# The end of a bidirectional scan and the start of its projection: side outputs of the last tile, the last scan unit and one tile's heads put at other places in the order

## The chip, the cores and the metric

The kernel runs on one core of one Trainium2 chip. The metric is the device time of one launch in microseconds (us); for the kernel before, three runs gave 2700.61, 2703.89 and 2706.90 us, so the median is 2703.89 us.

## What is computed

The reference is a small diffusion trunk with `DEPTH = 1`: 2048 latent tokens and 256 context tokens of width 1024 go through one HGRN2 mixer (a gated linear recurrence in both directions, 8 heads of 128) and one gated convolutional feed-forward block. Cut to what matters here:

```python
def hgrn2_chunk_scan(q, k, v, logf, s0):
    """S_t = diag(f_t) S_{t-1} + k_t v_t^T, o_t = S_t^T q_t"""
...
def hgrn2_mixer(h_ctx, h_lat, w_in, lb, g_gain, w_out, need_ctx):
    # q, zf_fwd, zf_bwd, v, g = split(h @ w_in, 5); f = lb + (1 - lb) * sigmoid(zf); k = 1 - f
    for d in range(2):
        oc_d, s_ctx = hgrn2_chunk_scan(... context, direction d, s0 = 0 ...)
        ol_d, _ = hgrn2_chunk_scan(... latents, direction d, s0 = s_ctx ...)
        o_l = o_l + _flip(ol_d, d, 2)
    def readout(o, g):
        o = rmsnorm(o, g_gain).transpose(0, 2, 1, 3).reshape(Bn, T, H * DV)
        return (o * jax.nn.silu(g)) @ w_out
...
lat = lat + g1 * yl
hl = modulate(rmsnorm(lat, norm_g[l, 1]), sh2, sc2)
lat = lat + g2 * conv_ffn(hl, ...)
return rmsnorm(lat, final_g)
```

So for each tile of 128 tokens and each head, the outputs of the two directions are added, normalised over the head's 128 values (sum of squares, power of minus one half, scale), multiplied by the silu of a gate, and the eight heads go through the output projection.

## The kernel before, in words

The latents are 16 tiles of 128 tokens (tiles 0 to 15). The scan (`mixer_scan`) runs over two groups `g` of eight tiles, in each over the eight heads `h`, and in each head over two units `u` of four tiles. The last thing that it does is therefore group 1, head 7, unit 1: tiles 12 to 15 of the last head.

**Ticks.** A projection of four tiles (512 columns) is eight steps of three matmuls (L943, L944, L945), each of 128 by 128 weights against 512 columns; the three are the high and low parts of a split product. One step is one tick of a clock. Everything else in the scan is put on an agenda, `at(tick, step)`, and is traced when the clock gets there. A head has two gate projections for each of its two units, 32 ticks in all. The last head has four more projections behind them (the output gates of heads 6 and 7, `out_gate`), so it has 64. Below, e+n is the n-th tick of head 7 in group 1. The traced order is not the last word: the compiler's scheduler orders each engine's instructions by its own cost model, and can issue a ready one ahead of one that it expects to wait. After that each engine takes its instructions strictly in order.

**A unit.** `gates` (ScalarE: L967, L969) makes the decay factors from a projection. `factors` then makes running products on VectorE (scans at L987; L998 to L1003) and small products on GpSimd (L1009 to L1031, `sd` at L1012 among them). At the ticks of the agenda follow `suffix` (two scans on VectorE, L1037, which wait for `sd`), `rest` (L1044 to L1052, L1021: the products `qp`, `qi`, `km`, `kd`, `ke` on VectorE), `scores` (TensorE: transposes of `kd` into the PSUM tag `tr`, L1075, and 48 small matmuls from `ke`, `km`, `qp`, L1119; then VectorE's masked copy L1136 and the sum `at` L1137), `stepped(0)` (matmuls `kv` L1150, states on VectorE L1153, copy `sk` on ScalarE L1158), `second` (`outputs(0)`, then `stepped(1)`) and `outputs(1)`. `outputs` writes `o` in PSUM (L1173 from the states, L1176 from `at`) and ScalarE copies it (`so`, L1181). The PSUM tag `o` has one buffer.

**Two directions.** The scan carries one direction's state (`Sf`) through the tiles. The other direction runs from tile 15 down to tile 0 in the projection phase (`mixer_out`): `heads(t)` multiplies the queries with the state `Sb` (`oi`, L841), adds to the stored output (L845), normalises, and moves `Sb` on by one tile (L852); `heads_T(t)` transposes, multiplies with the gates and splits (L880, L881, L80, L81); `residual(n, ...)` multiplies with the output weights (L1578 to L1580, 24 matmuls of 512 columns for each half). What passes from the scan to this phase goes through DRAM (`stash`), in four parts: state products `kv`, queries `q`, outputs and gates.

**Side outputs of tile 15.** For tile 15 the steps of `heads` and `heads_T` are done inside the scan, for heads 0 to 3, heads 4 and 5, and head 6 in turn, on data read back from the stash into one SBUF tile, `top`, with four parts (`kv`, `qb`, `o`, `g`):
- `load_top`: DMA from the stash (L1253, SP queue).
- `top_outputs`: matmuls `oi` (L1268) into the PSUM tag `o`, the one that the scan's own outputs use; VectorE adds it to `o` (L1270); ScalarE squares each head with a running sum, writing the squares over `oi` in PSUM (L1272); VectorE and GpSimd make the scale (L75, L76); VectorE moves `Sb` on (L1275).
- `top_scaled`: ScalarE multiplies by the scale (L1282).
- `top_turned`: transposes into the PSUM tag `tr` (L1289, also one buffer), VectorE's product with the gate (L1291), split (L80, L81).

Head 7 of tile 15 does the same in `last_out` and `last_turn`. `first_out` then holds tile 15's transposed and split outputs, and the projection phase begins with `residual(0, ...)` for tile 15, inside which `heads(14)` is traced.

Of the kernel before, what the change touches and what calls it, by code (L numbers as in the profile page):

```python
# [15 lines left out]
AF = mybir.ActivationFunctionType  # L16
# [29 lines left out]
def body(ctx, tc, a, out):  # L46
    nc = tc.nc
    pe, act, dve, pool, sp = nc.tensor, nc.scalar, nc.vector, nc.gpsimd, nc.sync
# [838 lines left out]
    clock, at, run, tick = ticking()  # L887
# [9 lines left out]
    def mixer_scan():  # L897
# [362 lines left out]
        def top_outputs(hs):  # L1260

            n, t = len(hs), NT - 1
            kv, qb, o, g = [top_part(i) for i in range(4)]
            ss, rs = [gp.tile([128, NH], F32, name=m, tag=m, bufs=2) for m in ("ss8", "rs8")]
            top_rs[hs] = rs
            oi = ps.tile([128, n, 128], F32, name="oi", tag="o")
            for j, h in enumerate(hs):
                pe.matmul(oi[:, j], qb[:, h], Sb[:, h], start=True, stop=True)  # L1268
            r = slice(hs[0], hs[-1] + 1)
            dve.tensor_tensor(o[:, r], o[:, r], oi, OP.add)  # L1270
            for j, h in enumerate(hs):
                act.activation(oi[:, j], o[:, h], AF.Square, accum_out=ss[:, j:j + 1])  # L1272
            rms_scale(rs[:, 0:n], ss[:, 0:n], n, 128)
            for h in hs:
                dve.scalar_tensor_tensor(Sb[:, h], Sb[:, h], decb[:, h, t:t + 1], kv[:, h],  # L1275
                                         OP.mult, OP.add)

        def top_scaled(hs):
            for j, h in enumerate(hs):
                o = top_part(2)[:, h]  # L1280
                with tc.issue_after(passed[-1]):
                    act.activation(o, o, AF.Copy, scale=top_rs[hs][:, j:j + 1])  # L1282

        def top_turned(hs):

            r = slice(hs[0], hs[-1] + 1)
            tp = ps.tile([128, len(hs), 128], F32, name="tp", tag="tr")
            for j, h in enumerate(hs):
                pe.transpose(tp[:, j], top_part(2)[:, h], ident)  # L1289
            g = top_part(3)[:, r]  # L1290
            dve.tensor_tensor(g, tp, g, OP.mult)  # L1291
            with tc.issue_after(passed[-1]):
                split(gls[0][:, r], gls[1][:, r], g)
# [45 lines left out]
        def head(g, h):  # L1339
            t0 = [HT * g, HT * g + UT]  # L1340
            last = g == 1 and h == NH - 1

            def ctx_gates():
                for d in range(2):
                    gates(d, h, None, project(weight(g, h, 2 - d), None))
                cv = values(cv_d[h // 2][:, h % 2])
                kd, sd, keys = factors(h, None, None, None, None)
                for dt, f in zip((5, 9, 12), (keys, *context_state(h, kd, sd, cv))):
                    at(clock[0] + dt, f)

            def gate(u):
                for d in range(2):
                    gates(d, h, u, project(weight(g, h, 2 - d), u))

            def unit(u, after):
                n = t0[u] // UT
                q = gp.tile([128, UT, 128], F32, name="q", tag="q", bufs=1)
                sp.dma_start(q, q_d[h][n])
                m, suffix, rest = factors(h, u, t0[u], q, values(v_d[h][n]))
                behind = (lambda: tied(rest)) if made_last else rest  # L1360
                for f, dt in zip((suffix, behind, *unit_steps(h, t0[u], m)), after):
                    at(clock[0] + dt, f)

            def out_gate(hh, u):
                keep_gate(hh, t0[u], swish(project(weight(g, hh, 4), u), ("q", "kdc")[hh % 2 ^ u]))

            if g == 0:
                ctx_gates()
            gate(0)
            unit(0, (6, 11, 19, 21, 24, 27) if last else (6, 11, 19, 21, 26, 31))  # L1370
            n = order.index((g, h)) + 1
            ahead = [(*order[n], ty) for ty in (2, 1)] if n < len(order) else \
                [(g, hh, 4) for hh in (NH - 2, NH - 1)]
            for i, w in enumerate(ahead):
                at(clock[0] + 2 + 7 * i, lambda w=w: weight(*w))
            gate(1)
            unit(1, (5, 9, 17, 19, 21, 23) if last else (6, 11, 19, 21, 26, 31))
            if last:
                c = clock[0]
                for k in range(4):  # L1380
                    at(c + 2 + k, lambda k=k: load_out_weight(k))
                for n, k in enumerate((4, 5, 6, 7)):
                    at(c + 8 + n, lambda k=k: load_out_weight(k))
                out_gate(NH - 2, 1)
                out_gate(NH - 2, 0)
                out_gate(NH - 1, 0)
                for k in range(4):
                    at(clock[0] + 1 + 2 * k, lambda k=k: split_out_weight(k))
                out_gate(NH - 1, 1)

        for g in range(2):
            for h in range(NH):
                c = clock[0]
                if g == 1 and h == 0:
                    tok.clear()
                    for kk, n in PLAIN.items():
                        sp.dma_start(block(*kk).bitcast(F32), tok_d[n])
                if g == 1 and h == 2:
                    at(c + 2, lambda now=c + 2: gate1(now))
                if g == 1 and 2 <= h < 6:  # L1400
                    for i in range(2):
                        at(c + 12 + 16 * i, lambda k=2 * (h - 2) + i, t=c + 12 + 16 * i: out_scaled(k, t))
                if g == 1 and h == NH - 2:
                    at(c + 36, lambda: load_top(range(6)))
                    for i, hs in enumerate(((0, 1, 2, 3), (4, 5))):
                        at(c + 44 + 10 * i, lambda hs=hs: top_outputs(hs))
                        at(c + 55 + 11 * i, lambda hs=hs: top_scaled(hs))
                        at(c + 65 + 9 * i, lambda hs=hs: top_turned(hs))
                if g == 1 and h == NH - 1:
                    hs = (NH - 2,)  # L1410
                    at(c + 35, lambda: load_top(hs, range(3)))
                    at(c + 42, lambda: top_outputs(hs))
                    at(c + 50, lambda: top_scaled(hs))
                    at(c + 48, lambda: load_top(hs, (3,)))
                    at(c + 57, lambda: top_turned(hs))
                head(g, h)
# [125 lines left out]
    def mixer_out(c3):  # L1542
# [128 lines left out]
        for t in range(NT - 1, -1, -1):  # L1671
            lat = next_lat
            steps = ()
            if prev is not None:
                xn = wn.tile([128, D], F32, name="xn", tag="xn", bufs=1)
                if t == NT - 2:
                    with behind_of(last_split[-1]):
                        steps = norm_steps(prev, xn)
                else:
                    steps = norm_steps(prev, xn)  # L1680
            if 1 < t < NT - 1:
                heads(t - 2, steps)
            else:
                for f in steps:
                    f()
            if 0 < t < NT - 1:
                next_lat = load_lat(t - 1)
            g = gs.pop(0)
            if t == NT - 1:
                residual(0, lat, *g, between={3: lambda: heads(t - 1)})  # L1690
                next_lat = load_lat(t - 1)
            else:
                residual(0, lat, *g, between={KT - 1 if t == NT - 2 else 1: turn} if t else {})
            if t == 1:
                load_rhs(1, "T2")
                for p in first:
                    p.load()
            if t == 0:
                for q, p in enumerate(first):
                    p.split("A11", hp.tile([128, 2, 4, 128], F32R, name="w", tag=("Sf", "Sb")[q],  # L1700
                                           bufs=1))
            residual(1, lat, *g, between={5: turn} if t == NT - 1 else
                     {} if t else {1: lambda: norm2(1, xn)})
            if t == NT - 1:
                heads(t - 2)
                sp.dma_start(conv[:, 0:V_CN], a["conv"])
            if t == 0:
                load_rhs(1, "T1")
            if prev is not None and t:
                norm2(t + 1, xn)  # L1710
            sp.dma_start(lat_d[t], lat)
            prev = lat
# [550 lines left out]
```

## Time and profile before

| what | value |
|---|---|
| median of three runs | 2703.89 us |
| the profiled execution's own time | 2705.35 us |
| its span (first to last instruction) | 2703.5 us |
| TensorE's mean granted clock | 0.995 |
| head 7 of group 1 begins (first step) | about 1124.3 us into the span |
| first matmul of the projection of tile 15 | 1203.56 us into the span |

All positions below are in us from the start of the span. A row of the timeline gives start, duration, engine, line, operation, out<-in, shapes, how often (merged), and in square brackets the engine's idle time before the row and what ended it. The view of waits gives who waited for whom, the total, the number of waits and the longest. The view of windows gives, for a stretch, its length and for each engine the busy time (and instructions), then the granted TensorE clock (PEclk), DMA's share and its GB/s.

### The profile page before, as it was taken

The numbers are of one execution on the slowest core, as the hardware profiler recorded it, in microseconds if no ns is written. First come the engines' busy times: TensorE is split into PE (matmuls) and PEld (weight loads), VectorE is DVE, ScalarE is ACT, GpSimd is POOL, SyncE is SP. The second block draws the span as 40 slices with busy tenths as digits, with TensorE's granted clock in tenths as the row PEclk, the third lists the DMA queues.
The fourth block names the chain that finished last, engine by engine and source line by source line (L and its number), as shares of the span: only waits on it lengthen the run. The fifth ranks groups of instructions, "written<-read, shape, count | busy, mean of one in ns | idle before, by whom it ended". The sixth has DMA issues, their size and how long they took to land.

```text
span 2703.5 us, 42065 instructions
## 1 busy us (share of the span) xinstructions
PE 2646.1 (98%) x15800; PEld 2205.9 (82%) x15800; DVE 2074.4 (77%) x2953; ACT 1187.3 (44%) x2051; POOL 597.9 (22%) x934
## 2 busy tenths in 40 slices
PE   7899999999999999999999999999999999999998
PEld 4787788888888888888887888888888888888887
DVE  4856766667887889878887878877887777578896
ACT  4645534433333233345566444443444444333444
POOL 1000222321222121111112444334433440000001
PEclk9999999999999999999999999999999999999999
DMA  8755655363445665548887322227232224888653
GB/s 341 276 198 195 233 197 183 102 248 120 151 152 175 217 204 180 163 138 310 294 315 278 107 81 94 86 71 296 94 94 68 86 81 159 301 283 285 206 180 133
DMA packets 257915, 498.12 MB, mean 184 GB/s; under 512 B 28192, under 2 KB 141232, under 8 KB 249136
## 3 DMA queue, kind: packets, MB, share of 16 engines
q1 hardware_dynamic: 252992, 486.20, 52.5%
q10 hardware_dynamic: 4720, 9.24, 0.9%
q8 instruction: 124, 2.03, 0.3%
q14 instruction: 79, 0.65, 0.1%
HBM read 335.70 MB, written 159.66 MB: 183 GB/s over the span
## 4 chain that ended last, share of the span: by engine, by line
PE 72%; DVE 10%; DMA 3%; POOL 1%; ACT 1%; issue 1%; SPq 0%; POOLq 0%; DVEq 0%; ACTq 0%
PE y L2076 4%; PE y L2075 4%; PE y L2077 4%; PE z L943 3%; PE z L945 3%; PE z L944 3%; PE zc L1474 3%; PE zc L1476 3%; PE zc L1477 3%; PE zd L1476 3%; PE za L1476 3%; PE za L1477 3%; PE zd L1477 3%; PE zd L1474 3%; PE za L1474 3%; PE y L1580 2%
## 5 line engine op out<-in xcount | busy, mean ns | idle before, releaser
L80 ACT ACTIVATE w<-raw 128x512 fp32r<-128x512 f32 (+1 forms) x286 | 186.1, 656 | 215.9 <-PE zd L1477 75.0
L81 DVE TENSOR_TENSOR w<-raw,w 128x512 fp32r<-128x512 f32 (+1 forms) x286 | 226.8, 797 | 64.3 <-ACT w L80 61.8
L81 DVE TENSOR_TENSOR w<-s,w 128x512 fp32r<-128x512 f32 x195 | 173.0, 892 | 81.8 <-ACT w L80 80.2
L2075 PE MATMUL y<-w,mh 128*128 128x512 f32 x600 | 233.4, 390 | 0.6 <-ACT X L2109 0.6
L2076 PE MATMUL y<-w,mh 128*128 128x512 f32 x600 | 233.5, 389 | 0.2 <-DVE w L81 0.2
L2077 PE MATMUL y<-w,ml 128*128 128x512 f32 x600 | 233.4, 389 | 0.0
L80 ACT ACTIVATE w<-s 128x512 fp32r<-128x512 f32 x195 | 121.7, 630 | 204.8 <-POOL s L220 82.5
L76 POOL TENSOR_TENSOR rs<-rs,mhalf 128x1 f32<-128x1 f32 (+3 forms) x53 | 58.2, 1102 | 446.5 <-DVE rs L75 433.9
L943 PE MATMUL z<-tok,w 128*128 128x512 f32 x352 | 145.6, 414 | 0.0
L1474 PE MATMUL zc<-rT,w 128*128 128x512 f32 x352 | 137.1, 389 | 1.9 <-DMA rT<-rhs1T 1.9
L945 PE MATMUL z<-tok,w 128*128 128x512 f32 x352 | 138.5, 394 | 0.0
L944 PE MATMUL z<-tok,w 128*128 128x512 f32 x352 | 138.0, 392 | 0.0
L1158 ACT ACTIVATE sk<-kv 128x256 f32<-128x256 f32 x64 | 24.6, 384 | 256.4 <-DVE states L1153 121.1
L1476 PE MATMUL zc<-rT,w 128*128 128x512 f32 x352 | 137.0, 389 | 0.0
L1477 PE MATMUL zc<-rT,w 128*128 128x512 f32 x352 | 136.9, 389 | 0.0
L219 POOL TENSOR_TENSOR s<-raw 128x512 f32<-128x512 f32 x54 | 90.6, 1677 | 194.9 <-DMA raw<-in_w_up_dram 128.7
L2075 PEld LDWEIGHTS y<-w,mh 128*128 128x128 f32 x600 | 112.6, 188 | 24.9 <-ACT X L2109 1.5
L2076 PEld LDWEIGHTS y<-w,mh 128*128 128x128 f32 x600 | 112.6, 188 | 23.8 <-DVE w L81 0.6
L2077 PEld LDWEIGHTS y<-w,ml 128*128 128x128 f32 x600 | 112.6, 188 | 23.6
L1476 PE MATMUL za<-rB,w 128*128 128x512 f32 x336 | 130.7, 389 | 0.0
L1477 PE MATMUL za<-rB,w 128*128 128x512 f32 x336 | 130.7, 389 | 0.0
L1474 PE MATMUL za<-rB,w 128*128 128x512 f32 x336 | 130.7, 389 | 0.0
(466 smaller groups left out, 7750.9 us busy)
## 6 DMA issues: line engine op xcount, KB each, us to landing
raw<-in_w_up_dram SPq DMA_DIRECT2D x88, 512.0 KB, 3.5
raw<-in_w_in_dram SPq DMA_DIRECT2D x75, 512.0 KB, 5.2
w<-w SPq DMA_DIRECT2D x32, 1024.0 KB, 6.1
lr<-m SPq DMA_DIRECT2D x49, 512.0 KB, 4.6
m<-r SPq DMA_DIRECT2D x66, 256.0 KB, 3.5
spare<-in_w_ada_dram SPq DMA_DIRECT2D x32, 512.0 KB, 5.1
kq<-stash SPq DMA_DIRECT2D x15, 1024.0 KB, 7.1
og<-stash SPq DMA_DIRECT2D x30, 512.0 KB, 5.1
```

What stands on the lines that cost most here:

```text
L80: i = act.activation(h, src, AF.Copy)
L81: j = dve.tensor_tensor(l, src, h.bitcast(F32), OP.subtract)
L219: eng.tensor_tensor(s1, a21, a22, OP.add)
L943: pe.matmul(z, w[:, 0, k], h, start=k == 0, stop=False, skip_group_check=True)
L944: pe.matmul(z, w[:, 0, k], l, start=False, stop=False, skip_group_check=True)
L945: pe.matmul(z, w[:, 1, k], h, start=False, stop=k == KT - 1, skip_group_check=True)
L1474: pe.matmul(o, w[:, 0, k], r[:, :, 0, k], start=start and k == 0, stop=False, skip_group_check=True)
L1476: pe.matmul(o, w[:, 0, k], r[:, :, 1, k], start=False, stop=False, skip_group_check=True)
L1477: i = pe.matmul(o, w[:, 1, k], r[:, :, 0, k], start=False, stop=k == 3, skip_group_check=True)
L2075: pe.matmul(z, lh, rh, start=start, stop=False, skip_group_check=True)
L2076: pe.matmul(z, lh, rl, start=False, stop=False, skip_group_check=True)
L2077: pe.matmul(z, ll, rh, start=False, stop=stop, skip_group_check=True)
```

## The change

No operation is added or taken away, and one operand changes. There are four edits:
1. `top_outputs` writes its squares over the query part of `top` in SBUF instead of over `oi` in PSUM.
2. The agenda of the side outputs moves: `top_outputs` is put two ticks behind the scan's own `outputs(1)`.
3. The last unit (head 7, unit 1) gets scores, states and outputs three ticks sooner.
4. `heads(14)` is traced behind the weights' second k-tile of tile 15's first half projection instead of behind the fourth.

In ticks of head 7:

| step | before | after |
|---|---|---|
| `outputs(1)` of head 6, unit 0; unit 1 | e+15; e+31 | e+15; e+31 |
| `top_outputs` heads 0-3; 4, 5; 6 | e+12; e+22; e+42 | e+17; e+33; e+45 |
| `top_scaled` | e+23; e+34; e+50 | e+28; e+39; e+51 |
| `top_turned` | e+33; e+42; e+57 | e+38; e+45; e+57 |
| `outputs(1)` of head 7, unit 0 | e+43 | e+43 |
| head 7, unit 1: scores; `stepped(0)`; `second`; `outputs(1)` | e+49; e+51; e+53; e+55 | e+46; e+48; e+50; e+52 |

```diff
             dve.tensor_tensor(o[:, r], o[:, r], oi, OP.add)
             for j, h in enumerate(hs):
-                act.activation(oi[:, j], o[:, h], AF.Square, accum_out=ss[:, j:j + 1])
+                act.activation(qb[:, h], o[:, h], AF.Square, accum_out=ss[:, j:j + 1])
             rms_scale(rs[:, 0:n], ss[:, 0:n], n, 128)
...
-            unit(1, (5, 9, 17, 19, 21, 23) if last else (6, 11, 19, 21, 26, 31))
+            unit(1, (5, 9, 14, 16, 18, 20) if last else (6, 11, 19, 21, 26, 31))
...
                     for i, hs in enumerate(((0, 1, 2, 3), (4, 5))):
-                        at(c + 44 + 10 * i, lambda hs=hs: top_outputs(hs))
-                        at(c + 55 + 11 * i, lambda hs=hs: top_scaled(hs))
-                        at(c + 65 + 9 * i, lambda hs=hs: top_turned(hs))
+                        at(c + 49 + 16 * i, lambda hs=hs: top_outputs(hs))
+                        at(c + 60 + 11 * i, lambda hs=hs: top_scaled(hs))
+                        at(c + 70 + 7 * i, lambda hs=hs: top_turned(hs))
...
-                    at(c + 42, lambda: top_outputs(hs))
-                    at(c + 50, lambda: top_scaled(hs))
+                    at(c + 45, lambda: top_outputs(hs))
+                    at(c + 51, lambda: top_scaled(hs))
                     at(c + 48, lambda: load_top(hs, (3,)))
...
-                residual(0, lat, *g, between={3: lambda: heads(t - 1)})
+                residual(0, lat, *g, between={1: lambda: heads(t - 1)})
```

In the first block of the agenda c is the start of head 6 (c + 32 is e), in the second it is e itself.

## The prediction

> **What bounds the kernel now.** I read the page first, then the view of waits for TensorE over 1110 to 1240 us, then each engine's timeline there.
>
> ```profile
> PE 2646.1 (98%) x15800; PEld 2205.9 (82%) x15800; DVE 2074.4 (77%) x2953; ACT 1187.3 (44%) x2051; POOL 597.9 (22%) x934
> ```
>
> TensorE (PE) is busy for 98% of the span and the change neither adds nor removes a matmul. So the time can move only by TensorE's idle time or by its clock. Its waits in the touched stretch:
>
> ```profile
> PE o L1173 <- ACT oi L1272: 3.9, 2, 3.0
> PE y L1578 <- ACT ghl L80: 1.4, 1, 1.4
> PE o L1176 <- DVE at L1137: 0.6, 1, 0.6
> PE tp L880 <- DVE og L866: 0.3, 1, 0.3
> ```
>
> The first is the largest: twice the scan's own outputs waited until ScalarE had squared the side outputs, because `oi` held the only buffer of the PSUM tag `o`. The longer wait, engine by engine:
>
> ```profile
> 1142.02 0.39 PE L943 MATMUL z<-tok,w 128*128 128x512 f32 x1
> 1145.82 0.49 PE L1173 MATMUL o<-states,qi 128*128 128x128 f32 x2 [2.95 <-ACT oi L1272]
> ...
> 1149.04 0.63 PE L943 MATMUL z<-tok,w 128*128 128x512 f32 x1
> ```
> ```profile
> 1141.42 0.32 DVE L1153 SCALAR_TENSOR_TENSOR states<-states,sd,kv 128x128 f32<-128x128 f32 x1
> ...
> 1143.31 0.68 DVE L1270 TENSOR_TENSOR top<-top,oi 128x512 f32<-128x512 f32 x1
> ```
> ```profile
> 1145.58 0.19 ACT L1272 ACTIVATION_READ_ACCUMULATOR oi<-top 128x1 f32 x1
> ```
>
> The last state that the outputs need was there at 1141.74. The buffer came free only at 1145.77, after VectorE's add and four squares. TensorE lost 2.95 us. The matmul at 1149.04 shows a second loss: 0.63 us where the same one takes 0.39 at 1142.02. The windows say why (PEclk is the number behind the five busy times):
>
> ```profile
> 1146.00:1148.00 2.00, 2.00 (x12) 1.76 (x13) 0.87 (x1) 1.97 (x6) 1.02 (x1) 0.80 0.01 2
> 1148.00:1150.00 2.00, 2.00 (x6) 1.54 (x6) 1.30 (x4) 0.56 (x2) 1.55 (x7) 0.50 0.66 195
> 1150.00:1152.00 2.00, 2.00 (x87) 1.63 (x89) 1.57 (x2) 0.60 (x1) 0.58 (x4) 0.85 0.00 0
> ```
> ```profile
> 1219.00:1223.00 4.00, 3.26 (x21) 2.76 (x22) 3.63 (x6) 2.63 (x5) 0.00 (x0) 1.00 1.02 418
> ```
>
> The granted clock was 0.80, 0.50 and 0.85 of full speed in the six microseconds behind the wait, which costs 0.4 + 1.0 + 0.3 = 1.7 us. Behind the wait of 1.4 us (the second of the list, which ends at 1219.67) it stayed at 1.00. So a long wait costs more than itself.
>
> **The change part by part.** The sum is made against the profiled execution: span 2703.5 us, its own time 2705.35, so 1.85 lies around the span, and it ran 1.46 us above the median of 2703.89. I apply the difference to the median.
>
> *Side outputs behind the scan's outputs (first group).* Outputs at e+15 now come before `oi` at e+17 and need only the state of 1141.74, about when TensorE ends the step that began at 1142.02. The 2.95 us go, and with them the clock's 1.7: **4.65 us**. The new danger is that `oi` waits for the copy `so`, which must empty the same buffer. It has two steps (1.36 us, by the rows below) for a copy of 256 columns; a gate's 0.60 us instruction could slip ahead of it. I take 0, with 0.5 as the bad end. The add, the `Sb` updates and the power go behind the next unit's `factors`: on GpSimd the power (L76) then stands behind that unit's small products instead of ahead. `top_outputs`, `top_scaled` and `top_turned` issue no DMA, so no SP instruction moves with them.
>
> *Third group (head 6).* The other part of that wait, 3.9 - 2.95, stands here, before `outputs(1)` at e+43:
>
> ```profile
> 1183.68 0.49 PE L1173 MATMUL o<-states,qi 128*128 128x128 f32 x2 [0.93 <-ACT oi L1272]
> ```
>
> With `oi` at e+45 it has nothing to wait for on ScalarE: **0.93 us**, without a clock dip (a shorter wait than the 1.4 us that had none).
>
> *Squares to SBUF.*
>
> ```profile
> L1282 ACT ACTIVATE top<-top,rs 128x128 f32<-128x128 f32 x7 | 2.3, 391 | 0.0
> L1272 ACT ACTIVATE oi<-top 128x128 f32<-128x128 f32 x7 | 2.0, 281 | 2.4 <-DVE top L1270 2.3
> ...
> L1300 ACT ACTIVATE y<-o 128x128 f32<-128x128 f32 x1 | 0.3, 277 | 0.1
> ```
>
> A square into PSUM takes 281 ns, the one square into SBUF (L1300, reading PSUM) 277, a scaled copy from SBUF to SBUF 391. So one square changes by -0.004 to +0.11 us, seven by at most 0.8. I take 0, because L1300 is the same operation; it is ScalarE time that TensorE no longer waits for. The Trainium skill speaks against this edit (ScalarE: Activation LUTs, Step-by-step: what each stage is for): it says ScalarE reaches PSUM faster than SBUF and advises PSUM as the destination. By it the bad end would hold, 0.8 us less gain if VectorE's L75, which waits for the squares in its queue, passed all of it on; the 277 against 281 does not bear it out.
>
> *The last unit three ticks sooner.* This is where the change can lose. Here is the stretch from e+32 on, first TensorE, then ScalarE, VectorE and GpSimd:
>
> ```profile
> 1166.44 0.60 PE L1289 MATMUL tp<-ident,top 128*128 128x128 f32 x4
> 1166.79 0.48 PE L943 MATMUL z<-tok,w 128*128 128x512 f32 x1
> ...
> 1168.27 0.60 PE L1075 MATMUL tr<-ident,kd 128*128 128x128 f32 x4
> ...
> 1170.49 0.48 PE L943 MATMUL z<-tok,w 128*128 128x512 f32 x1
> ...
> 1171.96 1.05 PE L1150 MATMUL kv<-v,kt 128*128 128x128 f32 x8
> 1172.77 0.48 PE L943 MATMUL z<-tok,w 128*128 128x512 f32 x1
> ...
> 1174.23 0.39 PE L943 MATMUL z<-tok,w 128*128 128x512 f32 x1
> 1174.91 0.38 PE L1173 MATMUL o<-top,qi 128*128 128x128 f32 x2
> ```
> ```profile
> 1165.94 0.60 ACT L967 ACTIVATE F<-z 128x512 f32<-128x512 f32 x1 [0.31 <-PE z L945]
> ```
> ```profile
> 1167.07 0.69 DVE L1291 TENSOR_TENSOR top<-tp,top 128x512 f32<-128x512 f32 x1 [3.00 <-PE tp L1289]
> ...
> 1169.79 0.68 DVE L81 TENSOR_TENSOR gh<-top,gh 128x512 fp32r<-128x512 f32 x1
> 1171.43 2.48 DVE L1037 TENSOR_TENSOR_SCAN S<-F,d 128x528 f32<-128x528 f32 x2 [0.96 <-POOL sd L1012]
> ...
> 1181.98 0.68 DVE L1021 TENSOR_TENSOR ke<-ke,rt 128x512 f32<-128x512 f32 x1
> ```
> ```profile
> 1158.21 3.41 POOL L76 TENSOR_TENSOR rs<-rs,mhalf 128x2 f32<-128x2 f32 x1 [7.57 <-DVE rs L75]
> ```
>
> The scores need `ke`. From the gate's start (1165.94, the projection of e+32) to the end of `ke` (1182.66) the chain over ScalarE, VectorE and GpSimd takes 16.7 us. TensorE's own work from e+32 to e+46 is 14 steps of 0.68 (1174.23 to 1174.91) = 9.5; the scores of unit 0, 2.22 (1168.27 to 1170.49); two `kv` and two `outputs` of eight 128-column matmuls, 4 x 0.81 (1171.96 to 1172.77) = 3.24; `oi` of heads 4 and 5, the transposes of heads 0 to 3, and `oi` of head 6 with the transposes of 4 and 5, 0.35 each (1166.44 to 1166.79) = 1.05. That is 16.0 us. So the slack that e+49 had is used up: the scores come 0.7 us too early if nothing else changes. And 0.69 + 0.68 = 1.37 us of VectorE work, the gate product and split of heads 0 to 3, leave a place with 3.00 us of idle time and come (e+38) into this chain: 2.1 us too early. Against it, TensorE can take steps ahead: at 1142.02 it did the 16th step before outputs due at the 15th, and three steps of the scores' former lead (2.0 us) have no other dependence. So this costs 0 to 2.1; I take **-0.5**. The work of heads 4 and 5 at e+33 (add, two `Sb` updates) fits into the idle 3.00 and 0.96 us. Behind the scores the spacing is the old one. The DMAs of the moved steps (two of `sk`, two of `so` on ScalarE's queue, two of `qi` on SP's) go 2 us sooner and pass no load.
>
> The wait for `at` (0.59 us, the third of the list) shrinks by the 0.35 us of `oi` for heads 4 and 5, which TensorE now does before it: **0.35 us**.
>
> *Heads of tile 14 sooner.*
>
> ```profile
> 1203.24 0.32 SPq L1550 DMA_DIRECT2D kq<-stash  x1
> ```
> ```profile
> 1203.56 0.39 PE L1578 MATMUL y<-wo,gh 128*128 128x512 f32 x1
> ...
> 1208.98 1.95 PE L841 MATMUL oi<-Sb,kq 128*128 128x128 f32 x16
> ...
> 1219.67 0.50 PE L1578 MATMUL y<-wo,ghl 128*128 128x512 f32 x1 [1.39 <-ACT ghl L80]
> ```
> ```profile
> 1198.53 0.37 ACT L1302 ACTIVATE y<-o,rs 128x128 f32<-128x128 f32 x1
> 1198.80 0.27 ACT L1181 ACTIVATE so<-o 128x128 f32<-128x128 f32 x1
> 1198.95 0.60 ACT L974 ACTIVATE kdc<-z 128x512 f32<-128x512 f32 x1
> ```
>
> `heads(14)` was traced behind the fourth k-tile, yet its `oi` ran only 5.4 us into the projection, twice the 2.7 us that the 12 matmuls of four k-tiles take (0.68 for three), because `kq` was only issued at 1203.24. Tracing it behind the second k-tile by itself gives nothing: **0**. What moves `kq` is the gate of head 7, unit 0, whose buffer it reuses. Its sigmoid (1198.95) stood behind the last unit's scaled output and copy, 0.37 + 0.27 us, and these now come three ticks sooner. So the heads' chain, on which the 1.4 us and 0.3 us waits of the second tile hang, can gain 0 to 0.64 us: **0.4**.
>
> Sum: 4.65 + 0.93 - 0.5 + 0.35 + 0.4 = **5.8 us**; 2703.89 - 5.8 = **2698.1 us** (2699.5 beside the profiled execution).
>
> **The rivals.**
> *The wait moves into the last unit's chain (slower).* One mechanism: GpSimd's power for heads 4 and 5, now traced right behind `factors` of unit 1, is issued ahead of that unit's small products, which `sd` and all of the chain wait for. Its price is the 3.41 us of the row at 1158.21. With 2.1 from above TensorE waits 5.5 us before the scores, and the clock dips as it did (1.7): 7.2. Against that stand 4.65 + 0.93 + 0.4, so the kernel is 1.2 us slower: 2705.1. It decides from a wait of 4.3 us on. For it: VectorE already idles 0.96 us for `sd` there. Against it: the traced order puts the small products first.
> *TensorE waits for `kq`.* If `oi` really stands behind the second k-tile, it is due at 1203.56 + 6 x 0.227 = 1204.9 and waits up to 4.1 us, with a dip of 1.7; the second tile's 1.4 + 0.3 are then gone. 4.1 less gain: 2702.2. Against it: the order followed the data before.
> *The dip is not the wait's.* Then only waits go: 5.8 - 1.7 = 4.1, 2699.8. For it: one place alone shows it here; against it: the clock falls right behind this wait and not behind the one of 1.4 us. The Trainium skill has the rule for it (TensorE: Matmul & The Clock Gate, Part 1: The HAM clock gate): half clock after an idle window of about 3.4 us, and by that a wait of 2.95 should leave the clock alone. This trace does not agree, with 0.50 behind 2.95 us.
> *More goes.* If also `at` (0.6) and the second tile's waits (1.4 + 0.3) vanish and the scores wait for nothing: 4.65 + 0.93 + 0.6 + 1.7 = 7.9, 2696.0.
>
> **How the numbers follow.** A measurement of this kernel can tell about 0.2% (5.4 us) from no change, so the line is at 2698.5. Chances: the forecast 0.50, with its own range 2696 to 2700 from the ends of the small terms, two thirds of it beyond the line (0.34); more goes 0.14; the chain 0.12, half of it worse than worked out, if unit 0's chain suffers too (0.06 slower); `kq` 0.12; the dip 0.06; no effect for another reason 0.06. Faster 0.34 + 0.14 = 0.48, slower 0.06, within 0.46. The range goes from 2694 (the largest gain and the 3 us by which runs differ from their median, in part) to 2703.5; beyond it lie the chain and half of no effect.
>
> **What would show it.** Right: no wait of L1173 for L1272; PEclk 1.00 through the scan's tail; the first projection matmul about 5.5 us earlier than 1203.56. Wrong: a wait before the last unit's L1075 or L1119 over 2 us, with L1037 waiting for `sd` longer than 0.96; a wait before L841; L1268 waiting for L1181; a second dip.

## The result and the profile after

The kernel after takes 2698.94 us in the median of 15 runs, the kernel before 2703.89 us in 15 runs beside them. The ratio is 0.9984 with a 95% interval of 0.9977 to 0.9990, so the change saves 4.3 us (2.7 to 6.2). The forecast was 2698.1 us. The profiled execution of after took 2697.74 us, with a span of 2695.8. One execution of after (9427.12 us), one of squares_only (4609.63) and the profiled one of later (2935.69) stand far outside all others, for a reason that no run shows, and are in no ratio and no reading below.

The page of after, first its busy times: TensorE's work is the same 15800 instructions, its busy time is 2.8 us less.

```profile
PE 2643.3 (98%) x15800; PEld 2205.0 (82%) x15800; DVE 2072.6 (77%) x2953; ACT 1188.0 (44%) x2051; POOL 599.6 (22%) x934
```

TensorE's waits from 1100 to 1240 us in after (who waits for whom: total, how often, the longest):

```profile
PE y L1578 <- ACT ghl L80: 1.4, 1, 1.4
PE tr L1075 <- ACT kt L1077: 0.5, 1, 0.5
PE o L1173 <- DVE states L1153: 0.4, 1, 0.4
PE tp L1289 <- ACT kt L1077: 0.3, 1, 0.3
```

The wait of L1173 for L1272 (3.9 us in two places) is gone, and so are those for `at` (0.6) and for `og` (0.3). Three waits are new, 0.5, 0.4 and 0.3 us. TensorE's timeline of after, at the places where those waits stood:

```profile
1138.27 0.38 PE L1173 MATMUL o<-states,qi 128*128 128x128 f32 x2
...
1140.84 1.05 PE L1268 MATMUL oi<-Sb,top 128*128 128x128 f32 x8
...
1145.51 0.66 PE L1075 MATMUL tr<-ident,kd 128*128 128x128 f32 x4 [0.52 <-ACT kt L1077]
...
1173.47 0.49 PE L1173 MATMUL o<-states,qi 128*128 128x128 f32 x2 [0.41 <-DVE states L1153]
```

The scan's outputs run without a wait, and the side outputs' `oi` follows 2.57 us behind them. The windows behind that place (PEclk is the number behind the five busy times) show the full clock, also in the third (1150 to 1152, 1.00), where before had 0.80, 0.50 and 0.85:

```profile
1146.00:1148.00 2.00, 2.00 (x14) 1.73 (x13) 2.00 (x3) 0.60 (x1) 1.43 (x1) 1.00 0.00 0
1148.00:1150.00 2.00, 2.00 (x13) 1.71 (x12) 1.93 (x4) 0.00 (x0) 0.00 (x0) 1.00 0.00 0
...
```

To compare executions I measure between four matmuls that every kernel has, so that what an execution loses elsewhere stays out: the first step of head 7 (e, at 1125.09 in before; the step at 1124.31 is still the last one of head 6), the step e+32, the first matmul of the projection (P15), and the first of tile 11's projection (P11). TensorE's timeline of after has them here:

```profile
1122.20 0.40 PE L943 MATMUL z<-tok,w 128*128 128x512 f32 x1
...
1158.51 0.40 PE L943 MATMUL z<-tok,w 128*128 128x512 f32 x1
...
1195.34 0.39 PE L1578 MATMUL y<-wo,gh 128*128 128x512 f32 x1
...
1258.48 0.48 PE L1578 MATMUL y<-wo,ghl 128*128 128x512 f32 x1
```

And in before (its P15 is the row at 1203.56 above):

```profile
1125.09 0.40 PE L943 MATMUL z<-tok,w 128*128 128x512 f32 x1
...
1165.74 0.40 PE L943 MATMUL z<-tok,w 128*128 128x512 f32 x1
...
1267.09 0.48 PE L1578 MATMUL y<-wo,ghl 128*128 128x512 f32 x1
```

From e to P11 before took 142.00 us and after 136.28: 5.72 us less. The same differences in all traces, in us ("dip" says that the clock fell to half for a while in that piece):

| kernel | edits in it | e to e+32 | e+32 to P15 | P15 to P11 | sum |
|---|---|---|---|---|---|
| before | none | 40.65, dip | 37.82 | 63.53 | 142.00 |
| before_again | none | 40.69, dip | 37.81 | 63.18 | 141.68 |
| heads_only | 4 | 39.22 | 37.80 | 63.31 | 140.33 |
| unit_only | 3 | 40.64, dip | 37.73 | 63.13 | 141.50 |
| squares_only | 1 | 38.59 | 37.61 | 63.56 | 139.76 |
| top_only | 2 | 35.87 | 36.92 | 64.19 | 136.98 |
| no_unit | 1, 2, 4 | 36.31 | 36.90 | 64.00 | 137.21 |
| no_squares | 2, 3, 4 | 35.86 | 36.82 | 63.28 | 135.96 |
| no_heads | 1, 2, 3 | 36.31 | 36.83 | 63.18 | 136.32 |
| after | 1 to 4 | 36.31 | 36.83 | 63.14 | 136.28 |
| later_again | 1 to 4, `oi` later | 36.54 | 36.80 | 65.26, dip | 138.60 |
| lat_first | 1 to 4, `lat` first | 36.29 | 36.82 | 66.97, dip | 140.08 |
| lat_mid | 1 to 4, `lat` second | 36.30 | 36.82 | 65.09, dip | 138.21 |

Executions of one order agree within 0.05 us in the first two columns, once a dip is set apart, and within about 0.35 us in the third (63.18 to 63.53 for before's order). Differences of some tenths can be read from this table; no timing of the whole kernel could show them.

### The profile page after: what moved, and what is told of

It is laid out like the page before. It is cut to its first block, busy times and chain, and to the rows that moved or that the text cites. A ratio compares the mean times of both kernels' runs of the same rounds, so it can differ in the third digit from the quotient of the medians.

```text
span 2695.8 us, 42069 instructions
## 1 busy us (share of the span) xinstructions
PE 2643.3 (98%) x15800; PEld 2205.0 (82%) x15800; DVE 2072.6 (77%) x2953; ACT 1188.0 (44%) x2051; POOL 599.6 (22%) x934
## 4 chain that ended last, share of the span: by engine, by line
PE 53%; DVE 1%; DMA 1%; issue 0%; ACT 0%; POOL 0%; SPq 0%; POOLq 0%; DVEq 0%; ACTq 0%
PE y L2076 5%; PE y L2077 5%; PE y L2075 5%; PE zc L1474 3%; PE zc L1477 3%; PE zc L1476 3%; PE za L1477 3%; PE zd L1477 3%; PE zd L1474 3%; PE zd L1476 3%; PE za L1476 3%; PE za L1474 3%; PE y L1580 2%; PE y L1578 2%; PE y L1579 2%; PE zb L1477 1%
## 5 line engine op out<-in xcount | busy, mean ns | idle before, releaser
L76 POOL TENSOR_TENSOR rs<-rs,mhalf 128x1 f32<-128x1 f32 (+3 forms) x53 | 57.4, 1086 | 431.2 <-DVE rs L75 407.3
L1474 PE MATMUL zc<-rT,w 128*128 128x512 f32 x352 | 137.6, 391 | 2.2 <-DMA rT<-rhs1T 2.2
L1474 PE MATMUL za<-rB,w 128*128 128x512 f32 x336 | 130.7, 389 | 0.0
```

The costliest lines, as they stand in the source:

```text
L1474: pe.matmul(o, w[:, 0, k], r[:, :, 0, k], start=start and k == 0, stop=False, skip_group_check=True)
```

## The experiments

The theory when they began: the time came from the waits for the buffer of `oi` and from the clock behind the longer one. The rivals: edit 1 alone frees ScalarE; edits 3 and 4 bring something themselves; the clock dips at random and has nothing to do with the wait.

**Edit 2 alone (top_only).**

```diff
-                        at(c + 44 + 10 * i, lambda hs=hs: top_outputs(hs))
-                        at(c + 55 + 11 * i, lambda hs=hs: top_scaled(hs))
-                        at(c + 65 + 9 * i, lambda hs=hs: top_turned(hs))
+                        at(c + 49 + 16 * i, lambda hs=hs: top_outputs(hs))
+                        at(c + 60 + 11 * i, lambda hs=hs: top_scaled(hs))
+                        at(c + 70 + 7 * i, lambda hs=hs: top_turned(hs))
...
-                    at(c + 42, lambda: top_outputs(hs))
-                    at(c + 50, lambda: top_scaled(hs))
+                    at(c + 45, lambda: top_outputs(hs))
+                    at(c + 51, lambda: top_scaled(hs))
```

> Only the agenda of the side outputs moves (second edit); squares stay in PSUM, the last unit and the heads of tile 14 stay. Measure: from the first step of head 7 to the first projection matmul of tile 11, 142.00 us before and 136.28 us with all four edits. Theory (the order behind the scan's outputs carries the gain): no wait of L1173 for the squares of heads 0 to 3, clock 1.00 behind it, 137 us or less, and 4 to 5 us less time. Rival (the squares' place in SBUF carries it, the order alone moves the wait to the next user of the buffer): a wait of L1173 or L1268 over 1.5 us remains and the stretch takes 140 us or more.

Measured: 2701.04 us, ratio 0.9993 (0.9984 to 1.0002), which alone would not tell it from no change. The trace does: e to P11 took 136.98 us, 3.35 less than the undipped execution of before's order (heads_only) and 5.02 less than before. Both waits for L1272 are gone. The agenda carries the gain. The last piece, 64.19, is the longest among the first ten rows of the table, which the run without edit 3 takes up below.

**Edit 1 alone (squares_only).**

```diff
-                act.activation(oi[:, j], o[:, h], AF.Square, accum_out=ss[:, j:j + 1])
+                act.activation(qb[:, h], o[:, h], AF.Square, accum_out=ss[:, j:j + 1])
```

> Only the squares go to SBUF (first edit). Theory (the buffer is held by add and squares in turn, and the clock falls because of the wait's length): L1173 still waits, but only for VectorE's add, which ended at 1143.99 against 1145.77 for the squares: 1.1 to 1.8 us instead of 2.95; the clock stays near 1.00; the stretch takes 138 to 139 us. Rival 1 (the dip is not the wait's): the clock falls all the same to about 0.5, 140 us. Rival 2 (squares in SBUF are slow): a square takes near 390 ns instead of 281.

Measured: 2699.98 us, ratio 0.9988 (0.9979 to 0.9997). TensorE's timeline of this run at the first group:

```profile
1141.47 0.49 PE L1173 MATMUL o<-states,qi 128*128 128x128 f32 x2 [1.85 <-DVE top L1270]
```

The buffer is now held until VectorE's add has read it, and no longer until the squares have: 1.85 us of wait in place of 2.95, and no dip behind it. So this edit by itself takes 1.1 us of the wait. The other two groups still wait for the add, 0.30 and 0.72 us, and e to P11 takes 139.76 us, a little more than the 138 to 139 expected. With edit 2 there is no such wait to shorten.

**Edit 3 alone (unit_only).**

```diff
-            unit(1, (5, 9, 17, 19, 21, 23) if last else (6, 11, 19, 21, 26, 31))
+            unit(1, (5, 9, 14, 16, 18, 20) if last else (6, 11, 19, 21, 26, 31))
```

> Only the last unit comes three ticks sooner (third edit). Theory (this edit gives nothing by itself and uses up slack): the two waits for the squares and the dip stay, 142 us plus 0 to 1.5 us in the stretch, with a new or longer wait before or in the last unit. Rival (it carries part of the gain, by clearing the end of the scan): 1 us or more less from the scan's end (head 7's step 48) to the first projection matmul of tile 14 than the 33.6 us of before minus the moved work, and 141 us or less in all.

Measured: 2701.25 us, ratio 0.9995 (0.9985 to 1.0004). Both waits for L1272 and the one for `at` stand, the expected new wait in the last unit does not come, and e to P15 takes 78.37 us (40.64 + 37.73) against 78.47 in before: the earlier scores neither cost nor bring anything there.

**Edit 4 alone (heads_only).**

```diff
-                residual(0, lat, *g, between={3: lambda: heads(t - 1)})
+                residual(0, lat, *g, between={1: lambda: heads(t - 1)})
```

> Only the heads of tile 14 are traced sooner (fourth edit). The order of instructions on each engine comes out the same as before, so every theory expects 0: 142.0 us in the stretch within 0.3, and the time of before. What it differs by is what two runs of one program differ by. The rival is that where buffers lie in memory matters: then the stretch or the median moves by over 1 us.

Measured: 2703.25 us, ratio 0.9996 (0.9987 to 1.0005). Every engine's instructions stand in the order of before, so this is a second measurement of before. It gave what I had not looked for. TensorE at the first group, and the windows behind:

```profile
1146.21 0.49 PE L1173 MATMUL o<-states,qi 128*128 128x128 f32 x2 [2.92 <-ACT oi L1272]
...
1147.90 0.39 PE L943 MATMUL z<-tok,w 128*128 128x512 f32 x1
```
```profile
1146.00:1148.00 2.00, 1.79 (x12) 1.66 (x13) 0.65 (x2) 1.97 (x7) 1.02 (x1) 1.00 0.00 0
1148.00:1150.00 2.00, 2.00 (x27) 1.54 (x29) 1.69 (x4) 1.05 (x5) 1.16 (x5) 1.00 0.72 193
```

The same wait, 2.92 us, and the clock stays at 1.00; the projection's matmul takes 0.39 us and not 0.63. What the dip costs this stretch is the difference of the first column, 40.65 - 39.22 = 1.4 us. That is most of the 1.67 us by which e to P11 is shorter here than in before; the rest lies in the last piece, within its spread. So the rival of the expectation, the place of the buffers in memory, is not needed to explain it.

**Before again (before_again).** The kernel before itself, unchanged, for a second profile.

> The kernel before, once more, for its trace. Its first profile shows the clock at 0.50 behind the wait of 2.95 us and a stretch of 142.00 us; the run with only the fourth edit, whose instruction order is the same, shows a wait of 2.9 us, no dip and 140.33 us. Theory (whether the clock falls behind a wait of this length depends on where it lies against something that runs freely): either 142.0 or 140.3 us within 0.2, the wait the same, nothing between. Rival (the dip grows with the wait): a value between, with a wait that differs by over 0.2 us.

Measured: 2705.01 us in one run. Its windows behind the wait, which was 2.94 us long:

```profile
1146.00:1148.00 2.00, 1.07 (x7) 1.07 (x8) 0.17 (x1) 1.90 (x7) 0.84 (x1) 0.89 0.00 0
1148.00:1150.00 2.00, 2.00 (x8) 1.61 (x7) 1.72 (x4) 1.70 (x6) 0.61 (x4) 0.50 0.19 47
1150.00:1152.00 2.00, 2.00 (x10) 1.58 (x8) 0.91 (x2) 0.06 (x1) 1.68 (x8) 0.76 0.49 150
```

The dip is back. Of four executions with this wait three dipped (before, before_again, unit_only) and one did not (heads_only).

**All but edit 3 (no_unit).** Edits 1, 2 and 4, with the line of edit 3 as in before.

> All edits but the third: the last unit stays at its old ticks. With the agenda edit alone, the scan ended sooner but the first projection tile took 16.89 us to the second tile's first matmul, against 15.89 with all four edits and 15.97 to 16.10 before. Theory (the third edit does not shorten the scan; it lets the last unit's results reach the projection in time, now that the scan ends 4 us sooner): without it that piece takes 16.6 us or more again, and the stretch from head 7's first step to tile 11 takes 136.8 to 137.4 us instead of 136.28. Rival (that 16.89 was chance): 15.9 to 16.1, and 136.3 or less, since the last unit's scores are then further from their operands.

Measured: 2701.07 us, ratio 0.9989 (0.9980 to 0.9998); e to P11 137.21 us, 0.93 more than after. The difference lies in the last piece (64.00 against 63.14, where executions of one order differ by up to 0.35). TensorE's waits of no_unit there:

```profile
PE y L1578 <- ACT ghl L80: 1.8, 1, 1.8
...
PE tp L880 <- DVE og L866: 0.3, 1, 0.3
```

With the scan's waits gone TensorE reaches the projection sooner than the heads of tile 14 are ready, and waits 0.4 + 0.3 us more for them than in after. The last unit three ticks sooner gives that back. Edit 3 is worth nothing alone and some 0.9 us beside edit 2, in the traces; by the ratios the two kernels cannot be told apart.

**All but edit 1 (no_squares).** Edits 2, 3 and 4, the squares again over `oi`.

> All edits but the first: squares stay in PSUM over oi. With all four edits TensorE waits 0.52 us for the copy kt (L1077), which stands behind four squares on ScalarE; with squares in PSUM the compiled order puts two of the squares behind that copy. Theory (with oi behind the scan's outputs nothing waits for the buffer, so the first edit is worth nothing there): no wait of L1173 for squares, 136.3 us within 0.5. Rival (the first edit matters in combination): a wait of L1173 or L1268 for L1272 of over 0.5 us and 137 us or more.

Measured: 2698.19 us, ratio 0.9982 (0.9973 to 0.9991); e to P11 135.96 us, 0.32 less than after, 0.45 less in the first piece and 0.14 more in the last. ScalarE's timelines say where the 0.45 come from, first after, then no_squares:

```profile
1143.70 0.31 ACT L1272 ACTIVATE top<-top 128x128 f32<-128x128 f32 x1 [1.90 <-DVE top L1270]
...
1144.01 0.29 ACT L1272 ACTIVATE top<-top 128x128 f32<-128x128 f32 x1
...
1144.59 0.29 ACT L1272 ACTIVATE top<-top 128x128 f32<-128x128 f32 x1
1144.79 0.18 ACT L1272 ACTIVATION_READ_ACCUMULATOR top<-top 128x1 f32 x1
1144.89 0.57 ACT L1077 ACTIVATE kt<-tr 128x512 f32<-128x512 f32 x1
```
```profile
1147.10 0.28 ACT L1272 ACTIVATE oi<-top 128x128 f32<-128x128 f32 x1 [1.90 <-DVE top L1270]
...
1147.54 0.28 ACT L1272 ACTIVATE oi<-top 128x128 f32<-128x128 f32 x1
1147.75 0.19 ACT L1272 ACTIVATION_READ_ACCUMULATOR oi<-top 128x1 f32 x1
1147.85 0.58 ACT L1077 ACTIVATE kt<-tr 128x512 f32<-128x512 f32 x1
1148.32 0.27 ACT L1272 ACTIVATE oi<-top 128x128 f32<-128x128 f32 x1
```

In after all four squares stand ahead of the copy `kt`, which must empty `tr` before the next transposes: the copy starts 1.19 us behind the first square, and L1075 waits 0.52 us. In no_squares the compiler put the copy behind two squares: 0.75 us, and no wait. So edit 1 in this company costs the scan a little, by the order that it leads to. The ratios of the two kernels do not separate them.

**Side outputs still later (later, later_again).** All four edits, and `top_outputs` three ticks further back for the first group, so that the copy `kt` would stand ahead of the squares.

```diff
-                        at(c + 49 + 16 * i, lambda hs=hs: top_outputs(hs))
+                        at(c + 52 + 13 * i, lambda hs=hs: top_outputs(hs))
```

> All four edits, and the side outputs of heads 0 to 3 another three ticks later, at e+20, behind the next scores. Theory (with all four edits a new wait of 0.52 us, 0.7 with its start, came in before the scores' second transposes, because the squares stand ahead of the copy kt on ScalarE): it goes, and the stretch takes 135.4 to 135.8 us instead of 136.28. Rival (the work only moves to where VectorE is late): the wait for at or the states grows by as much, 136.3 or more.

> All four edits with the side outputs of heads 0 to 3 at e+20, once more, for a trace: the earlier one fell into an execution with a mean clock of 0.848. Theory: no wait before the scores' second transposes at e+19, 135.4 to 135.8 us for the stretch instead of 136.28. Rival: the wait for at or the states grows, 136.3 or more.

Measured: later 2698.15 us, ratio 0.9979 (0.9970 to 0.9988); later_again, the same kernel for its trace, 2702.27 us in one run. L1075 no longer waits for `kt`, but L1173 waits for the states once more, and the first piece is 36.54, 0.23 more than in after. The projection's wait grew from 1.4 to 2.0 us, and there the clock dipped:

```profile
1215.92 0.50 PE L1578 MATMUL y<-wo,ghl 128*128 128x512 f32 x1 [1.98 <-ACT ghl L80]
```
```profile
1216.00:1218.00 2.00, 2.00 (x8) 1.61 (x9) 1.78 (x3) 0.65 (x2) 0.00 (x0) 0.57 1.02 416
1218.00:1220.00 2.00, 2.00 (x13) 2.00 (x12) 0.69 (x1) 1.52 (x3) 0.00 (x0) 0.57 1.07 442
```

The new wait is removed, and the trace wins nothing by it; by the ratios later and after cannot be told apart.

**The load of `lat` sooner (lat_first, lat_mid).** What remains is the 1.4 us before `ghl` (a part of tile 14's split outputs). In after VectorE stands 0.98 us at L1587 for the load of `lat`, and the product that `ghl` needs (L881) is behind it. lat_first puts that load ahead of the stash loads, lat_mid behind the second of them:

```diff
+        next_lat = load_lat(NT - 1)
         load_stash(0, 2, NT - 2)
         load_stash(2, 1, NT - 2)
         load_stash(3, 1, NT - 2)
...
-        next_lat = load_lat(NT - 1)
```
```diff
         load_stash(0, 2, NT - 2)
         load_stash(2, 1, NT - 2)
+        next_lat = load_lat(NT - 1)
         load_stash(3, 1, NT - 2)
...
-        next_lat = load_lat(NT - 1)
```

> All four edits, and the first tile of the residual stream is loaded ahead of the stash of tile 14 instead of behind it. The wait of the second tile (1.4 us, L1578 for the split of tile 14) ended behind VectorE's L1587, which waited for that load. Theory (that load sets the end of the wait): L1587 runs early, the wait falls to under 0.8 us, the stretch to 135.3 to 135.8. Rival (the gates' load through the stash, or the chain of tile 14's heads, ends as late): the wait stays at 1.2 us or more, 136.2 to 136.8; or the queries' load, now behind this one, comes later and it is longer.

> All four edits, and the first residual tile is loaded behind the queries and outputs of tile 14, but ahead of its gates, which wait for their own store. Loading it ahead of the queries made these late: the stretch took 140.08 us. Theory (VectorE's L1587, waiting for this load, holds up the split that the second tile waits for): here the queries are as early as with four edits, L1587 has its data early, and the wait of 1.4 us falls below 0.9; 135.4 to 135.9 us. Rival (the gates of tile 14, loaded only after their store has landed, end as late): 1.3 us or more, 136.2 to 136.6.

Measured: lat_first 2701.72 us, ratio 0.9999 (0.9990 to 1.0007); lat_mid 2699.45 us, 0.9978 (0.9969 to 0.9988). TensorE in lat_first, then in lat_mid:

```profile
1213.46 1.09 PE L880 MATMUL tp<-ident,og 128*128 128x128 f32 x8 [0.77 <-DVE og L866]
...
1215.44 3.33 PE L841 MATMUL oi<-Sb,kq 128*128 128x128 f32 x16 [0.89 <-DMA kq<-stash]
```
```profile
1210.07 0.50 PE L1578 MATMUL y<-wo,ghl 128*128 128x512 f32 x1 [0.52 <-ACT ghl L80]
...
1211.98 3.65 PE L841 MATMUL oi<-Sb,kq 128*128 128x128 f32 x16 [1.18 <-DMA kq<-stash]
```

In lat_first the loads behind the one moved ahead come later, and TensorE waits for `kq` and `og`: 3.83 us more than after in the last piece, up to 1.7 of them a dip behind these waits. In lat_mid the wait for `ghl` shrinks to 0.52 as meant, but the next tile's `kq` comes later: a new wait of 1.18, with a dip. The last piece is 1.95 us longer in this trace, of which 1.7 is the price of a dip (worked out in the last section). The ratio is not worse than after's. If other executions of lat_mid don't dip there, the two agree; no second trace of it was taken, so this stays open. The intervals of lat_mid, later, no_squares and after overlap, so none of them is a version to prefer.

**All but edit 4 (no_heads).** Edits 1, 2 and 3; the order of every engine is that of after.

> All of the change but edit 4 (heads of tile 14 stay traced behind the fourth k-tile). The order of the instructions on every engine is the same as in the kernel after, so my theory (edit 4 moves nothing, and the clock dip behind the 2.95 us wait is gone because the wait is) expects the stretch from the first step of head 7 to the first projection matmul of tile 11 at 136.0 to 136.6 us (136.28 in the kernel after), no dip of the clock in the scan's tail, and a ratio of 0.998 to 0.999 to the kernel before. Rival: edit 4 is worth the 0.4 us that I put there; then the stretch has 136.7 or more, in the distance from the first matmul of the projection on (78.4 us from the first to tile 11 in the kernel after less the scan's part). A ratio of 0.999 or more would say that the difference between the two kernels is within what chips and batches do by themselves.

Measured: 2698.77 us, ratio 0.9979 (0.9971 to 0.9988). e to P11 took 136.32 us, against 136.28 in after. Edit 4 does nothing, and the gain is measured a second time: 5.7 us (3.2 to 7.8), with 4.3 (2.7 to 6.2) the first time.

## Why the prediction was right

The forecast of 2698.1 us lies 0.8 us below the measured median. The 5.4 us that the prediction took for the least that runs can tell from no change was too much: the interval of 2.7 to 6.2 tells 4.3 us from nothing. The sum stood against the profiled execution of before, and there it holds closely: 5.8 us predicted, 5.72 found between e and P11. The main mechanism was right, the closeness is partly luck: the clock's term was 0.3 too large for this execution, and the -0.5 stands where other waits came. By its terms:

- **First group, 2.95 + 1.7.** The wait of 2.92 us went, as said. That the first column differs by as much between executions without a dip (39.22 - 36.31 = 2.9) is in part chance: the new wait of 0.52 us for `kt` stands in this piece, and 0.36 us of `oi`, that of heads 4 and 5, has left it for the middle one. From e to P15 the waits and gaps of TensorE fell by 3.3 us (4.74 in heads_only, 1.43 in after) and its busy time by 0.6. The clock's part is not a fixed cost. It was 1.4 us of this stretch in three of four executions with the wait and nothing in the fourth, so on average about 1.1. It belonged to the execution that I had, which is why 5.8 fits that one; from an undipped execution the change saves 140.33 - 136.28 = 4.05. The measured 4.3 and 5.7 lie at and above that. The rival "the dip is not the wait's" (4.1 us, 2699.8) fails as a mechanism, since no trace without the wait of 2.9 us has a dip at this place, but what it would have given is within the measured interval.
- **Third group 0.93, `at` 0.35, scores -0.5**, together 0.78. The middle column gives 37.82 - 36.83 = 0.99, though the 0.36 us of `oi` came into it. The 0.93 went but 0.41 came back as a wait for the states (L1153) and 0.27 as one of L1289 for `kt`; the wait for `at` vanished whole (0.6 and not 0.35). The scores came without any wait: no row of L1075 or L1119 of the last unit has one, nor has L1037 more than 1.03 for `sd`. So the -0.5 was wrong: I had added up TensorE's steps to 16.0 us against a chain of 16.7 and taken the difference for a wait. In after TensorE took 18.03 us from e+32 (1158.51) to these scores, 0.68 of them in the two new waits; the chain, from the gate's start at 1158.71 to the end of `ke` at 1175.88, took 17.2, so `ke` was there 0.66 us before TensorE came to it. unit_only, with the same three ticks, shows 78.37 against 78.47 us to P15.
- **Squares 0.** Wrong in sign by a little: 0.3 us lost in the traces, through the order of `kt` and the squares, not through the price of a square.
- **Tail +0.4.** 63.53 - 63.14 = 0.39, but before's own executions spread from 63.18 to 63.53, so this is no confirmation. The mechanism was wrong: the sigmoid `kdc` does come 0.3 us sooner relative to P15, yet `kq` is issued 0.31 us before P15 as it was 0.32 before. ScalarE's four issues of `kdc` stand between and took 2.36 us instead of 1.92. What edit 3 does here is seen only against kernels without the waits: 0.9 us (no_unit against after).
- **Edit 4, 0.** Right: heads_only and no_heads leave every engine's order as it is without it.

The end of the chain on VectorE and the first of the last unit's scores on TensorE, in after:

```profile
1175.18 0.70 DVE L1021 TENSOR_TENSOR ke<-ke,rt 128x512 f32<-128x512 f32 x1
```
```profile
1176.54 0.60 PE L1075 MATMUL tr<-ident,kd 128*128 128x128 f32 x4
```

The rival with the slower ending, GpSimd's power ahead of the small products, did not happen; in after `sd` of the last unit runs at 1163.40 and L76 for heads 4 and 5 starts behind it, as the traced order said:

```profile
1163.40 0.21 POOL L1012 TENSOR_TENSOR sd<-TB,S 128x8 f32<-128x8 f32 x1
...
1163.82 1.65 POOL L76 TENSOR_TENSOR rs<-rs,mhalf 128x2 f32<-128x2 f32 x1
```

`oi` at L841 runs 5.42 us into the projection in after as in before (1200.76 - 1195.34), so the `kq` rival did not happen either. Open is why top_only's ratio (0.9993) is smaller than its trace (5.0 us less than before, 3.4 less than the undipped order) lets expect; its interval holds the 3.4 but not the 5.0.

## What to carry to other kernels

When two users share the only buffer of a tag, put the one that the main chain does not wait for behind the other, and look at what its slower release then meets: here three waits of 0.3 to 0.5 us came in place of 4.8. A gap's price in one profile can hold a part that another execution does not have; before it goes into a sum, look for the same gap in a second execution. Small edits of one tail are compared between fixed instructions of the trace, since the ratios of whole runs could not rank them.

## What the runs showed of the hardware

**A dip of the clock lasts whole pieces of 3.41 us, and where the borders of these pieces lie decides whether a wait is followed by one.** Three windows around the dip, 2 us wide, lose 2 x (0.20 + 0.50 + 0.15) = 1.7 us in before and 2 x (0.11 + 0.50 + 0.24) = 1.7 in before_again: 3.41 us at half clock, or nothing, as in heads_only. Dips stand at other places too. In before two more begin at 321.18 and 601.07 us, and this one at 1147.20; the distances between them, 279.89 and 546.13 us, are 82 and 160 times 3.4133 us. So the time of an execution can be cut into such pieces from any of its dips. Here are the piece ahead of the dip and its own in before, then the same two in heads_only, counted from its dip at 1465.22 (behind the length stands TensorE's busy time):

```profile
1143.79:1147.20 3.41, 1.38 (x10) 1.34 (x11) 1.29 (x5) 3.01 (x11) 1.02 (x1) 1.00 0.13 38
1147.20:1150.61 3.41, 3.41 (x11) 2.55 (x10) 2.28 (x5) 1.36 (x5) 2.10 (x10) 0.50 0.39 115
```
```profile
1144.37:1147.78 3.41, 1.57 (x11) 1.49 (x12) 1.29 (x5) 3.20 (x12) 1.02 (x1) 1.00 0.12 38
1147.78:1151.19 3.41, 3.41 (x109) 2.87 (x108) 2.29 (x5) 1.77 (x6) 2.12 (x10) 1.00 0.46 120
```

The waits are equally long, but the border falls elsewhere in them: TensorE was busy for 1.38 us of the piece ahead in before, for 0.62 in before_again and 0.76 in unit_only, and half clock followed; in heads_only it was busy for 1.57, and none did. A wait for a DMA in the next phase (L1474), which the change does not touch, shows it more clearly. First no_heads, then squares_only:

```profile
1462.12 0.50 PE L1474 MATMUL zc<-rT,w 128*128 128x512 f32 x1 [2.42 <-DMA rT<-rhs1T]
```
```profile
1459.70:1463.11 3.41, 0.99 (x4) 0.85 (x5) 3.25 (x4) 2.34 (x2) 0.10 (x1) 1.00 1.01 432
1463.11:1466.52 3.41, 3.41 (x9) 2.68 (x9) 0.20 (x1) 1.24 (x2) 0.00 (x0) 0.50 0.95 393
```
```profile
1461.35 0.50 PE L1474 MATMUL zc<-rT,w 128*128 128x512 f32 x1 [2.47 <-DMA rT<-rhs1T]
```
```profile
1457.31:1460.72 3.41, 1.57 (x7) 0.95 (x6) 2.75 (x3) 1.41 (x2) 0.00 (x0) 1.00 0.95 394
1460.72:1464.13 3.41, 2.79 (x12) 2.33 (x13) 1.60 (x2) 2.80 (x3) 0.10 (x1) 1.00 0.98 417
```

In no_heads the whole wait lies in one piece, and the dip follows; in squares_only a wait as long lies across the border at 1460.72, and none does. Over all pieces at full clock in the 13 traces, from 130 us to shortly before the end, half clock followed each of the 23 in which TensorE was busy for less than 1.56 us, and none of those with more than 1.94; in between it followed 7 and did not follow 12, and what decides there is not shown. The length of one gap alone does not tell: at L1474 the 13 traces had gaps of 1.61, 1.65, 1.89, 1.97, 2.06, 2.09, 2.47 and 2.49 us without a dip, and of 2.21, 2.24, 2.42, 2.45 and 2.93 us with one. A dip can also last longer: the one at 598.24 in heads_only takes two pieces. The borders lie elsewhere in each execution, and no run shows what sets them; for a single execution the dip is therefore a matter of chance.

This corrects the prediction, which said that the trace does not agree with the Trainium skill (TensorE: Matmul & The Clock Gate, Part 1: The HAM clock gate): the page has a window of about 3.4 us that runs freely, and half clock after an idle one. The length of the pieces and their fixed grid in each execution agree with it. The window need not be idle, though: in before TensorE was busy for 1.38 of the 3.41 us, and there the measurement decides.

**A square into SBUF is longer by itself and shorter in a row.** One takes 0.29 to 0.31 us in after against 0.28 into PSUM in no_squares, but the next starts 0.31 us later (1143.70 to 1144.01) against 0.44 (1147.10 to 1147.54). The Trainium skill (ScalarE: Activation LUTs, Step-by-step: what each stage is for) calls PSUM the faster destination; the single row agrees by 0.02 us, the pitch with its accumulator read does not.
